# A block of two layers on one core: the second FFN's up-projection by Strassen's algorithm, in a written order

## The chip, the cores and the metric

The kernel runs on one core of a Trainium2 chip. The metric is the device time of one execution, in microseconds (us). The median of three runs before the change is 1634.23 us (1628.58 to 1636.04). The trace is that of one profiled execution, whose span from the first to the last instruction is 1633.7 us.

The engines are TensorE (PE in the profile; PEld is its weight load), VectorE (DVE), ScalarE (ACT), GpSimd (POOL), and SyncE (SP), whose queue issues the DMAs. Each engine works through its own list of instructions in order; semaphores tie the lists together.

## The reference

Two layers work on 512 tokens `x` and 256 context tokens `ctx`, 1024 features wide, in float32: a Fourier and Hyena mixer with an FFN, then latent attention with an FFN. The change touches the FFN of the second layer, and the norm ahead of it:

```python
D_MODEL, SEQ, D_FF = 1024, 512, 2816

def _conv_ffn(h, w_up, conv_w, conv_b, w_down):
    gate, val = jnp.split(h @ w_up, 2, axis=-1)
    return (jax.nn.silu(_dwconv3(gate, conv_w, conv_b)) * val) @ w_down
...
x = x + g1 * yx
x = x + g2 * _conv_ffn(_modulate(_rms_norm(x, norm2[i]), sh2, sc2), *ffn)
```

`_dwconv3` is a convolution of three taps over the tokens, feature by feature.

## The kernel before

Features lie on the 128 partitions, tokens on the free axis. `x`, `hh` and `hl` are lists of 8 tiles of 128 x 512. Precision is kept by splitting each operand of a matmul into a high part, rounded to the type fp32r by ScalarE (`hi`, line 131), and a low part, the difference, by VectorE (`lo`, line 137). `mm3` (lines 156 to 160) then runs three matmuls into one accumulator: high by high, weights' high by low, weights' low by high. Each has a weight tile of 128 x 128 of its own.

A weight tile comes by `wload`: a DMA of 128 x 1024 into `wr`, its high part into `wh`, its low part into `wl`. These three tags have three buffers each in the pool `W`, in turn; so a high part is made when TensorE is through with the tile that had the buffer. PSUM has three buffers of 1024 columns (`mm`) and two of 512 (`ms`).

The second FFN has 2816 = 22 x 128 hidden features. `up(f)` in `ffn` (line 1156) loads a gate tile and a value tile of weights, runs 8 x 2 `mm3` over the 8 tiles of `hh` and `hl` (48 matmuls of 512 columns), then the convolution on the gate straight from PSUM (lines 373 to 375, one ScalarE and two VectorE instructions), the Silu on ScalarE, the product with the value on VectorE, and the split into `ah` and `al`. For f = 0 the matmuls run in two halves of 256 tokens. The down-projection (`res_proj`, line 1102) comes in three groups of 8, 8 and 6 hidden tiles: for each of 8 output tiles a weight load, 24 or 18 matmuls of 512 columns, and one VectorE addition to `x` (line 1143). The first tile of the next group is computed ahead of each group.

Ahead of the FFN stands the attention's output projection, `res_proj` over two halves of 256 tokens, with weights loaded again for the second half where they were not kept. The norm of a half (`norm`, line 254) hangs on it by hooks: squares on ScalarE, their sum, `fold` (a matmul with ones), a reciprocal root on VectorE in twelve small steps, `spread` (a matmul that brings it to all partitions), and for each tile `scaled` (VectorE, then ScalarE with the bias, which writes `hh`) and `low` (VectorE, which writes `hl`).

In the mixer the order of the engines is written out by hand (`manual_schedule`); elsewhere, the second FFN among it, a scheduler sets the order on each engine by the order in the program and what is ready.

## Time and profile before

| | |
|---|---|
| median of three runs | 1634.23 us |
| the profiled execution's span | 1633.7 us |
| TensorE clock granted, mean | 0.989 |
| weights of the second FFN's up-projection | 44 loads of 512 KB |
| of its down-projection | 16 loads of 512 KB, 8 of 384 KB |
| landing of one such load after its issue | 3.0 to 3.3 us, median |

In a row of the timeline stand the start, the duration (both us), the engine, the line, the operation, the tile written and those read, the shape, and how many like it follow; in brackets, idle time of the engine before it and what ended that. TensorE's durations overlap, since matmuls are pipelined: its pace is the distance of two starts. The same holds for VectorE to a small degree. A group's row gives the count, then the busy time, the mean in ns, and idle time ahead. Times in the trace count from the span's start.

### The profile page before, as it was taken

To read this page: it belongs to the slowest core of one execution; us is meant where nothing else is said; L and a number is where in the kernel's file an instruction comes from. 1 tells how busy PE (TensorE), PEld (TensorE's weight loads), DVE (VectorE), ACT (ScalarE), POOL (GpSimd) and SP (SyncE) were. 2 spreads that over 40 slices of the span, in tenths; PEclk is the share of its full clock that TensorE was granted. 3 is DMA by queue.
4 is the path that set the end of the run, shared out by engine and by line. 5 is a ranking of instruction groups with operands and counts; after the bars stand their busy time and mean duration, and the time that the engine had idled before them with its cause. 6 is when DMAs were issued, how large, how long until landed. Compare 5 with 4: busy or idle time off the path is not lost.

```text
span 1633.7 us, 20802 instructions
## 1 busy us (share of the span) xinstructions
PE 1590.5 (97%) x8248; PEld 1300.4 (80%) x8248; DVE 1047.7 (64%) x1702; ACT 620.7 (38%) x883; POOL 109.5 (7%) x165
## 2 busy tenths in 40 slices
PE   7999998999999999999999989999999999999999
PEld 5787888888888888888888877666659888878887
...
PEclk9999998999999999999999998999999999999999
...
GB/s 361 109 105 231 156 29 78 192 118 112 159 155 117 77 129 145 164 104 77 113 160 86 83 70 1 13 11 14 0 99 147 78 103 92 90 104 90 90 91 90
DMA packets 54541, 173.35 MB, mean 106 GB/s; under 512 B 6187, under 2 KB 9453, under 8 KB 53421
## 3 DMA queue, kind: packets, MB, share of 16 engines
...
q8 instruction: 65, 1.06, 0.2%
...
## 4 chain that ended last, share of the span: by engine, by line
PE 81%; DVE 14%; issue 2%; ACT 1%; POOL 1%; DMA 1%; SPq 0%; POOLq 0%; DVEq 0%; ACTq 0%
PE mm L158 24%; PE mm L159 23%; PE mm L160 23%; PE pv L1611 2%; DVE wl L138 1%; DVE S L1587 1%; DVE junk L243 1%; PE s L1557 1%; DVE wr L1626 1%; PE k L158 1%; PE k L160 1%; PE k L159 1%; DVE hl L313 1%; PE mm L616 1%; DVE mx L1571 0%
## 5 line engine op out<-in xcount | busy, mean ns | idle before, releaser
L158 PE MATMUL mm<-hh,wh 128*128 128x512 f32 (+2 forms) x1360 | 481.7, 357 | 1.8 <-ACT wh L133 0.9
L159 PE MATMUL mm<-hl,wh 128*128 128x512 f32 (+2 forms) x1360 | 479.3, 353 | 2.3 <-DVE hl L313 2.3
L160 PE MATMUL mm<-hh,wl 128*128 128x512 f32 (+2 forms) x1360 | 478.7, 353 | 1.6 <-DVE wl L138 1.6
L133 ACT ACTIVATE wh<-wr 128x1024 fp32r<-128x1024 f32 (+1 forms) x192 | 197.8, 1033 | 571.1 <-PE mm L159 547.9
L138 DVE TENSOR_TENSOR wl<-wr,wh 128x1024 fp32r<-128x1024 f32 (+2 forms) x192 | 231.0, 1205 | 236.2 <-ACT wh L133 229.6
L158 PEld LDWEIGHTS mm<-hh,wh 128*128 128x128 f32 x1360 | 257.5, 190 | 48.7 <-issue 7.8
L159 PEld LDWEIGHTS mm<-hl,wh 128*128 128x128 f32 x1360 | 257.8, 190 | 39.0 <-DVE hl L313 3.5
L160 PEld LDWEIGHTS mm<-hh,wl 128*128 128x128 f32 x1360 | 257.6, 190 | 37.6 <-DVE wl L138 2.2
L243 DVE SCALAR_TENSOR_TENSOR junk<-wr,sb 128x1024 bf16<-128x1024 f32 x128 | 156.2, 1220 | 40.4 <-DMA wr<-wmodT 39.8
L158 PE MATMUL mm<-ah,wh 128*128 128x512 f32 (+1 forms) x480 | 172.4, 359 | 0.0
L160 PE MATMUL mm<-ah,wl 128*128 128x512 f32 (+1 forms) x480 | 172.2, 359 | 0.0
L159 PE MATMUL mm<-al,wh 128*128 128x512 f32 (+1 forms) x480 | 172.0, 359 | 0.0
L1143 DVE SCALAR_TENSOR_TENSOR xr<-mm,mod,xr 128x512 f32<-128x512 f32 (+1 forms) x100 | 61.7, 631 | 154.8 <-PE mm L160 153.1
L159 PEld LDWEIGHTS mm<-al,wh 128*128 128x128 f32 x480 | 90.5, 189 | 14.1 <-DVE al L138 0.2
L158 PEld LDWEIGHTS mm<-ah,wh 128*128 128x128 f32 x480 | 90.4, 188 | 14.2 <-issue 0.3
L160 PEld LDWEIGHTS mm<-ah,wl 128*128 128x128 f32 x480 | 90.4, 188 | 14.2
L1611 PE MATMUL pv<-S,V 128*128 128x512 f32 x192 | 93.9, 598 | 2.5 <-ACT S L1590 2.5
L1175 ACT ACTIVATE fg<-fg 128x772 f32<-128x772 f32 (+1 forms) x44 | 32.6, 741 | 97.7 <-DVE fg L375 90.9
L1565 ACT ACTIVATE S<-s,rks 128x512 f32<-128x512 f32 x96 | 62.6, 685 | 12.4 <-PE pv L1611 8.5
L1611 PEld LDWEIGHTS pv<-S,V 128*128 128x128 f32 x192 | 34.5, 190 | 34.7 <-issue 29.3
L1587 DVE TENSOR_TENSOR S<-S,mx 128x1536 f32<-128x1536 f32 x32 | 55.3, 1749 | 2.3 <-POOL mx L1583 2.3
L1583 POOL PARTITION_ALL_REDUCE mx<-mx x16 | 44.9, 2804 | 163.6 <-DVE mx L1580 163.6
...
## 6 DMA issues: line engine op xcount, KB each, us to landing
wr<-w_up SPq DMA_DIRECT2D x88, 512.0 KB, 3.2
wr<-wmodT SPq DMA_DIRECT2D x80, 512.0 KB, 3.2
wr<-w_dn SPq DMA_DIRECT2D x32, 512.0 KB, 3.3
...
wr<-w_in SPq DMA_DIRECT2D x16, 512.0 KB, 4.2
wr<-w_out SPq DMA_DIRECT2D x13, 512.0 KB, 3.3
...
wr<-w_o SPq DMA_DIRECT2D x11, 512.0 KB, 3.2
```

Of the source, the lines that this page charges most:

```text
L133: self.nc.scalar.activation(dst, src, AF.Copy)
L138: (eng or self.nc.vector).tensor_tensor(dst, src, hi.bitcast(F32), op=ALU.subtract)
L158: mmul(out, wh, xh, start=start, stop=False)
L159: mmul(out, wh, xl, start=False, stop=False)
L160: mmul(out, wl, xh, start=False, stop=stop)
L243: nc.vector.scalar_tensor_tensor(junk, raw, 1.0, self.sb[:, j, :], op0=ALU.mult, op1=ALU.mult, accum_out=acc)
L1143: nc.vector.scalar_tensor_tensor(x[m][:, a2:b2], ps[:, a2:b2], mod[:, 8 * sec + m, c : c + 1], x[m][:, a2:b2], op0=ALU.mult, op1=ALU.add)
L1175: nc.scalar.activation(g[:, :n], g[:, :n], AF.Silu)
L1565: nc.scalar.activation(c.S[a][j // 3][:, j % 3, :], c.ps[a, j], AF.Copy, scale=c.r[:, g : g + 1])
L1583: nc.gpsimd.partition_all_reduce(c.m[a][:, 1, :], c.m[a][:, 0, :], P, bass.bass_isa.ReduceOp.max)
L1587: v.tensor_tensor(c.S[a][h], c.S[a][h], mb.to_broadcast([P, 3, T]), op=ALU.subtract)
L1611: nc.tensor.matmul(c.P[a], V[:, j, o : o + 128], c.S[a][j // 3][:, j % 3, :], start=j == 0, stop=j == 5)
```

## The change

The first 2 of the 22 up tiles are computed as before. For the other 20, Strassen's algorithm takes the place of the 8 block products: the reduction is cut into two halves of 512 features (a), the tokens into two halves of 256 (b), and the outputs are gate (g) and value (v). Seven products `P1` to `P7` of 4 `mm3` each (12 matmuls of 256 columns) use sums of weight blocks and sums of blocks of the norm's result. The sums of weights (`S1` to `S4`, 512 columns each) are made by VectorE for each tile, then split (`Ha`, `La`, `Hb`, `Lb`). The sums of the norm's result (`T1` to `T4`, `Th`, `Tl`) are made once. For this `scaled` in `norm` writes the whole result, in float32, into "quarter" tiles first, by one more ScalarE instruction, and `hh` and `hl` from that. The products are added up by VectorE from PSUM (`C1` to `C4`, `Ua`, `Ub`, `Xv`, 256 columns each) with one copy by ScalarE (`K1`); gate and value then lie in SBUF.

All steps of this FFN stand in one written order, in which TensorE, VectorE, ScalarE and SP each take their steps as they come. A step's name ends in its up tile, or in its group and output tile. `R` is a DMA, `H` a high part, `L` a low part; `Ca`, `Cb`, `Cc` are the convolution, `Si` the Silu, `Ml` the product with the value, `Ah` and `Al` the split; `U1` is the second whole tile, `D` a down tile, `X` its addition to `x`. The down-projection is cut into five groups of 5, 5, 4, 4 and 4 hidden tiles, between the ups. The first two up weights are loaded in a hook of the output projection, ahead of the load for its last tile, m=4. The first whole tile U0 is run around the second half's norm, in the code ahead of the string.

On every engine the instructions up to the last loads of the output projection stand in the same order as before. TensorE has 720 matmuls more.

```diff
+UP_ORDER = """
+Rv2 Rg2 Rv3 Hv2 S1.2 T1 Hg2 U1 Ca0 Lv2 Th1 S2.2 Tl1 Ha2 T3 La2 Th3 T2 S3.2 Th2 Tl3 S4.2 Tl2 Hb2 Rg3 Cb0 Lb2 P1.2 Ca1 Cc0 P2.2 T4 K1.2 Si0 Lg2 P5.2 Th4
+C1.2 Rv4 Ml0 Hv3 P6.2 Tl4 Ah0 Lv3 P7.2 Ua2 S1.3 P1.3 Ub2 Xv2 C2.2 P4.2 K1.3 S2.3 S3.3 Ha3 P3.2 Cb1 Hg3 S4.3 La3 P2.3 Rg4 Hb3 Cc1 P5.3 Hv4 Lb3 Si1 P6.3
+C1.3 Lv4 P7.3 Ml1 Lg3 Ah1 P1.4 Ua3 Rv5 C3.2 Ub3 Xv3 P4.3 C2.3 S1.4 C4.2 P3.3 S2.4 Hg4 S3.4 K1.4 Ha4 Lg4 P2.4 S4.4 La4 Hb4 Rg5 Hv5 C1.4 P5.4 Lb4 Rv6 Lv5
+P6.4 Al0 P7.4 C3.3 Ca2 Ua4 S1.5 P1.5 Cb2 Ub4 Cc2 P4.4 Xv4 Si2 C2.4 S2.5 P3.4 Hg5 C4.3 Ml2 Ha5 P2.5 S3.5 K1.5 La5 Ah2 S4.5 P5.5 C1.5 Hb5 Rg6 Lg5 P6.5
+Al1 Hv6 Lb5 Rv7 Ca3 Lv6 P7.5 Ua5 Cb3 P1.6 Ub5 Cc3 P4.5 Xv5 Si3 C2.5 C3.4 S1.6 P3.5 Hg6 C4.4 S2.6 K1.6 P2.6 Ml3 Ha6 S3.6 Ah3 Lg6 La6 S4.6 P5.6 C1.6 Hb6
+Rg7 Al2 P6.6 C3.5 Hv7 Lb6 Rd0.0 Ca4 Lv7 P7.6 Ua6 Cb4 P1.7 Ub6 Cc4 P4.6 Xv6 Si4 C2.6 S1.7 P3.6 C4.5 Hg7 S2.7 K1.7 Ml4 Ha7 P2.7 S3.7 Ah4 Al3 La7 Ca5 S4.7
+P5.7 C1.7 Hb7 Rd0.1 Al4 P6.7 Lg7 Hd0.0 Lb7 Rd0.2 Hd0.1 Ld0.0 P7.7 Ua7 Rv8 Cb5 D0.0 Xv7 Cc5 Ub7 Si5 C4.6 C2.7 Ca6 Ld0.1 C3.6 Rg8 P4.7 Ml5 X0.0 Ah5 Cb6
+P3.7 C4.7 Cc6 Hg8 D0.1 S1.8 Si6 S3.8 Hd0.2 S2.8 Hv8 Ld0.2 Lv8 Rd0.3 D0.2 S4.8 Ha8 X0.1 Rd0.4 La8 Lg8 C3.7 Rv9 P1.8 Ml6 Hb8 X0.2 Ah6 P2.8 Al5 K1.8 Lb8
+Ca7 P5.8 Hd0.3 C1.8 Cb7 Ld0.3 P6.8 Cc7 Rg9 Al6 P7.8 Si7 Ua8 Hd0.4 Ml7 D0.3 Xv8 Ah7 Ub8 Ld0.4 C2.8 Rd0.5 S1.9 S3.9 S2.9 P4.8 Al7 S4.9 P3.8 X0.3 Hg9 C4.8
+Lg9 Ca8 D0.4 C3.8 Hv9 Cb8 Ha9 Cc8 Lv9 Si8 La9 Rd0.6 P1.9 Hb9 Rd0.7 X0.4 P2.9 Lb9 K1.9 Ml8 P5.9 Hd0.5 C1.9 Ah8 Ld0.5 P6.9 Al8 Rv10 P7.9 Hd0.6 Ua9 Xv9
+Ld0.6 D0.5 Ub9 Rg10 C2.9 S1.10 P4.9 X0.5 S2.10 P3.9 S3.10 Hg10 C4.9 S4.10 Ca9 D0.6 Lg10 Hd0.7 C3.9 Hv10 Ld0.7 Cb9 Rv11 Lv10 D0.7 Ha10 X0.6 Rg11 Cc9
+La10 Si9 Rv12 Ml9 S1.11 P1.10 Ah9 X0.7 Hb10 S2.11 P2.10 K1.10 Lb10 P5.10 Al9 Hv11 C1.10 S3.11 P6.10 Lv11 P7.10 S4.11 Ha11 Ua10 Rg12 Xv10 P1.11 La11
+Ub10 P4.10 K1.11 C2.10 S1.12 P3.10 S2.12 Hg11 C4.10 Lg11 Ca10 P2.11 C3.10 Hb11 Rd1.0 Cb10 P5.11 Cc10 Hv12 Lb11 Si10 P6.11 C1.11 Lv12 P7.11 Ha12 Ua11
+S3.12 P1.12 Xv11 Ub11 La12 P4.11 K1.12 C2.11 S4.12 P3.11 Ml10 Hg12 Rd1.1 C4.11 Ah10 Lg12 P2.12 Ca11 C3.11 Rd1.2 Hb12 Cb11 Al10 P5.12 Hd1.0 Lb12 P6.12
+C1.12 Ld1.0 P7.12 Cc11 Rd1.3 Hd1.1 Ua12 Si11 Ld1.1 D1.0 Ub12 Rv13 Xv12 C2.12 Ml11 Ah11 Al11 P4.12 X1.0 P3.12 C4.12 Ca12 D1.1 Cb12 Hd1.2 C3.12 Hd1.3
...
+Al21 D3.7 Hd4.1 X3.6 Ld4.1 Rd4.4 D4.0 Hd4.2 X3.7 Ld4.2 Rd4.5 D4.1 Hd4.3 X4.0 Ld4.3 Rd4.6 D4.2 Hd4.4 X4.1 Ld4.4 Rd4.7 D4.3 Hd4.5 X4.2 Ld4.5 D4.4 Hd4.6
+X4.3 Ld4.6 D4.5 Hd4.7 X4.4 Ld4.7 D4.6 X4.5 D4.7 X4.6 X4.7
+"""
+UP_GROUPS = ((0, 5), (5, 10), (10, 14), (14, 18), (18, 22))
+UP_WHOLE = 2
...
         def scaled(d):
             A, B = self.A[i][k][:, j, :], self.mod[i][:, 24 * k : 24 * k + 8, j]
+            if whole is not None:
+                u = box[d] = whole(d)
+                nc.vector.scalar_tensor_tensor(u, x[d][:, c0 : c0 + n], A[:, d : d + 1], box["R"][:, :n], op0=ALU.mult, op1=ALU.mult)
+                nc.scalar.activation(u, u, AF.Identity, bias=B[:, d : d + 1])
+                return nc.scalar.activation(hh[d][:, c0 : c0 + n], u, AF.Copy)
...
+        def whook(stage, j, m):
+            hook(stage, j, m)
+            if stage and j == 6:
+                first.extend(self.wload(I["w_up"][1, 0, q]) for q in range(2))
...
-        self.ffn(1, x, hh, hl, T, [(0, T)], half, None)
+        self.ffn_blocks(x, hh, hl, quarter, first, rest.steps)
...
+        def S1(f):
+            s, g = self.t(bl, [P, 1024], F32, "sum"), k_["rg", f]
+            k_["sa", f] = s
+            v.tensor_tensor(s[:, 512:1024], g[:, 0:512], g[:, 512:1024], op=ALU.add)
...
+        def prod(ps, w, o, mov):
+            for q in range(4):
+                s = slice(o + 128 * q, o + 128 * q + 128)
+                self.mm3(ps, w[0][:, s], w[1][:, s], *mov(q), q == 0, q == 3)
...
+        def P1(f):
+            m = k_["m", f] = self.mm()
+            prod(m[:, 0:256], k_["wv", f], 0, part(0, 0))
+        def P2(f):
+            prod(k_["m", f][:, 512:768], k_["wv", f], 512, part(1, 0))
+        def P5(f):
+            b = k_["b", f] = self.ms()
+            prod(b[:, 0:256], k_["wa", f], 512, tf(1))
+        def P6(f):
+            prod(k_["m", f][:, 0:256], k_["wa", f], 0, tf(2))
+        def P7(f):
+            prod(k_["m", f][:, 512:768], k_["wb", f], 512, tf(3))
+        def P4(f):
+            prod(k_["m", f][:, 0:256], k_["wg", f], 0, tf(4))
+        def P3(f):
+            prod(k_["b", f][:, 0:256], k_["wb", f], 0, part(1, 1))
+        def K1(f):
+            k_["t", f] = self.t(bl, [P, 3, 256], F32, "t")
+            nc.scalar.copy(k_["t", f][:, 0, :], k_["m", f][:, 0:256])
...
+        def C1(f):
+            k_["v", f] = self.t(tm, [P, T], F32, "fv", 3)
+            plus(k_["v", f][:, 0:256], k_["t", f][:, 0, :], k_["m", f][:, 512:768])
+        def Ua(f):
+            plus(k_["t", f][:, 1, :], k_["t", f][:, 0, :], k_["m", f][:, 0:256])
+        def Ub(f):
+            plus(k_["t", f][:, 2, :], k_["t", f][:, 1, :], k_["m", f][:, 512:768])
+        def Xv(f):
+            plus(k_["v", f][:, 256:512], k_["t", f][:, 1, :], k_["b", f][:, 0:256])
+        def C2(f):
+            k_["g", f] = self.t(tm, [P, T], F32, "fg")
+            minus(k_["g", f][:, 256:512], k_["t", f][:, 2, :], k_["b", f][:, 0:256])
...
+        with self.tc.manual_schedule(engines={ENG.PE, ENG.DVE, ENG.Activation, ENG.SP}):
+            k_["wg", 0], k_["wv", 0] = first
+            take(KD)
+            Rv(1)
+            Rg(1)
+            Hv(1)
+            Hg(1)
+            U_(0, [(0, 256)], (0, 1))
+            f2(False, 0)
+            U_(0, [(0, 256)], (2, 3, 4, 5))
+            Lv(1)
+            Lg(1)
+            f2(False, 1)
+            U_(0, [(0, 256)], (6, 7))
+            for d in range(KD + 1):
+                if d < KD:
+                    a2(d, 0)
+                if d:
+                    a2(d - 1, 1)
+            U_(0, [(256, 256)], range(KD))
+            for s in UP_ORDER.split():
+                step(s)
```

More of the change, by code (lines that the diff above doesn't have):

```diff
@@ L251, in make_A, with norm @@
             self.nc.vector.scalar_tensor_tensor(self.A[i][k][:, j, a:b], sc, 1.0, self.pcol[:, o + a : o + b], op0=ALU.add, op1=ALU.mult)
-    def norm(self, i, k, x, hh, hl, c0, n, tp):
+    def norm(self, i, k, x, hh, hl, c0, n, tp, whole=None):
         nc = self.nc
@@ L311, in low @@
         def low(d):
+            if whole is not None:
+                return nc.vector.tensor_tensor(hl[d][:, c0 : c0 + n], box.pop(d), hh[d][:, c0 : c0 + n].bitcast(F32), op=ALU.subtract)
             B = self.mod[i][:, 24 * k : 24 * k + 8, j]
@@ L1717, in layer1 @@
         self.xp = self.pool("xres")
[L1718 removed]
+        tp = lambda: self.t(nt, [P, 256], F32, "nt")
         x = [self.t(self.xp, [P, T], F32, f"xr{d}") for d in range(KD)]
@@ L1728, in layer1 @@
         hl = [self.t(hp, [P, T], F32R, f"hl{d}") for d in range(KD)]
-        hook, rest = self.norm_hook(*[self.norm(1, 1, x, hh, hl, c, 256, tp) for c in (0, 256)])
-        self.res_proj(1, 2, oh, ol, KD, lambda m: I["w_o"][m], x, half, hook, ready=2)
-        rest()
+        quarter = [[None] * 2 for _ in range(2)]
+        for a, b in ((0, 0), (0, 1), (1, 1), (1, 0)):
+            quarter[a][b] = self.t(self.xp, [P, 4, 256], F32, "quarter", 5)
+        whole = lambda b: lambda d: quarter[d // 4][b][:, d % 4, :]
+        hook, rest = self.norm_hook(*[self.norm(1, 1, x, hh, hl, 256 * b, 256, tp, whole(b)) for b in range(2)])
+        first = []
+        def whook(stage, j, m):
+            hook(stage, j, m)
+            if stage and j == 6:
+                first.extend(self.wload(I["w_up"][1, 0, q]) for q in range(2))
+        self.res_proj(1, 2, oh, ol, KD, lambda m: I["w_o"][m], x, half, whook, ready=2)
         self.close("pO")
```

177 lines of the change are left out of this document (176 added, 1 removed).

## The prediction

> **What bounds the kernel now.** I read the page first, then the stretches of the second FFN, then single rows of TensorE and VectorE there.
>
> ```profile
> span 1633.7 us, 20802 instructions
> ...
> PE 1590.5 (97%) x8248; PEld 1300.4 (80%) x8248; DVE 1047.7 (64%) x1702; ACT 620.7 (38%) x883; POOL 109.5 (7%) x165
> ...
> PE   7999998999999999999999989999999999999999
> ...
> PEclk9999998999999999999999998999999999999999
> ...
> PE 81%; DVE 14%; issue 2%; ACT 1%; POOL 1%; DMA 1%; SPq 0%; POOLq 0%; DVEq 0%; ACTq 0%
> ```
>
> TensorE is busy 97% of the span and holds 81% of the chain that ended last. In the second FFN it is the bound outright; in the table of stretches (span, then TensorE, weight loads, VectorE, ScalarE, GpSimd busy, clock, DMA share, GB/s) the first row is the stretch after the first up tile, the next two are one up tile each:
>
> ```profile
> 1276.00:1630.30 354.30, 353.83 (x1526) 285.43 (x1524) 151.20 (x177) 106.48 (x130) 0.00 (x0) 1.00 0.28 95
> ...
> 1311.15:1322.31 11.16, 11.16 (x50) 8.95 (x49) 5.06 (x6) 3.94 (x6) 0.00 (x0) 1.00 0.27 94
> 1322.31:1333.47 11.16, 11.16 (x50) 8.95 (x49) 5.06 (x6) 3.94 (x6) 0.00 (x0) 1.00 0.27 96
> ```
>
> TensorE has no gap in 354 us, while VectorE works 151 us and ScalarE 106. An up tile is 48 matmuls of 512 columns and takes 11.16 us, VectorE 5.06 us of it. So less TensorE work shortens this stage one for one, until VectorE is asked for more than TensorE takes.
>
> **The change, part by part. Matmuls.** Twenty up tiles go from 48 matmuls of 512 columns to 7 products of 12 matmuls of 256. Such matmuls run already in the attention output projection; these are the first and the last of 97 rows in a row:
>
> ```profile
> 1229.01 0.28 PE L158 MATMUL mm<-Oh,wh 128*128 128x256 f32 x1
> ...
> 1240.41 0.28 PE L158 MATMUL mm<-Oh,wh 128*128 128x256 f32 x1
> ```
>
> 11.40 us over 96 steps is 0.1187 us each, with the borders between weight tiles in it. 84 of them are 9.97 us (one product 1.425), so a tile saves 1.19 and twenty save **23.8 us**. The down-projection keeps its 528 matmuls of 512 columns; eight tiles per group become eight tiles in each of five shorter groups. Its pace, by the starts of the additions that end two neighbouring tiles of 24 matmuls in the first and in the second group:
>
> ```profile
> 1374.27 0.75 DVE L1143 SCALAR_TENSOR_TENSOR xr<-mm,mod,xr 128x512 f32<-128x512 f32 x1 [2.92 <-PE mm L160]
> ...
> 1379.87 0.75 DVE L1143 SCALAR_TENSOR_TENSOR xr<-mm,mod,xr 128x512 f32<-128x512 f32 x1 [3.52 <-PE mm L160]
> ...
> 1502.63 0.75 DVE L1143 SCALAR_TENSOR_TENSOR xr<-mm,mod,xr 128x512 f32<-128x512 f32 x1 [0.19 <-PE mm L160]
> ...
> 1508.12 0.75 DVE L1143 SCALAR_TENSOR_TENSOR xr<-mm,mod,xr 128x512 f32<-128x512 f32 x1 [2.80 <-PE mm L160]
> ```
>
> 5.60 and 5.49 us, a mean of 0.231 us a matmul; the sum is 122 us before and after, and costs nothing new.
>
> **VectorE.** A Strassen tile adds four weight sums, three 1024-wide low parts instead of two (and one of 512), and seven additions of 256 columns out of PSUM. What counts is the step from one instruction to the next when VectorE has a queue:
>
> ```profile
> 1256.13 0.48 DVE L1143 SCALAR_TENSOR_TENSOR xr<-mm,mod,xr 128x256 f32<-128x256 f32 x1
> 1256.53 0.47 DVE L308 SCALAR_TENSOR_TENSOR nt<-xr,A,ms 128x256 f32<-128x256 f32 x1
> ...
> 1258.51 0.42 DVE L274 TENSOR_TENSOR nt<-nt,nt 128x256 f32<-128x256 f32 x1
> 1258.85 1.22 DVE L138 TENSOR_TENSOR wl<-wr,wh 128x1024 fp32r<-128x1024 f32 x1
> ...
> 1260.06 1.22 DVE L138 TENSOR_TENSOR wl<-wr,wh 128x1024 fp32r<-128x1024 f32 x1
> 1261.19 0.15 DVE L283 SCALAR_TENSOR_TENSOR nrm_s<-ms,nrm_s 128x2 f32<-128x2 f32 x1
> ...
> 1281.94 0.69 DVE L1177 TENSOR_TENSOR fg<-fg,mm 128x512 f32<-128x512 f32 x1 [0.72 <-ACT fg L1175]
> 1282.61 0.75 DVE L374 SCALAR_TENSOR_TENSOR fg<-mm,pcol,fg 128x511 f32<-128x511 f32 x1
> 1283.39 0.69 DVE L138 TENSOR_TENSOR al<-fg,ah 128x512 fp32r<-128x512 f32 x1
> 1284.00 0.74 DVE L375 SCALAR_TENSOR_TENSOR fg<-mm,pcol,fg 128x511 f32<-128x511 f32 x1
> ```
>
> So 256 columns step 0.40 from PSUM and 0.34 from SBUF, 1024 from SBUF 1.135, 512 from PSUM 0.665, 512 from SBUF 0.605 (640 columns, in between, 0.74). A tile is 3 x 1.135 + 9 x 0.605 (four sums, one low part, two convolution taps, the product, its low part) + 7 x 0.40 = **11.65 us on VectorE against 9.97 on TensorE**. A down tile is the reverse: 1.3 to 1.4 us on VectorE, 12 or 15 matmuls, 2.8 or 3.5 us, on TensorE. Hence, where ups follow each other without downs, VectorE sets the pace. I sum both engines along the written order. Ahead of the product P7.7 (tile 7, the last before the first down tile) TensorE has U1 and 39 products: 11.16 + 39 x 1.425 = 66.7 us. It needs Lb7, and VectorE has up to there 26 x 1.135 + 44 x 0.605 + 6 x 0.665 + 34 x 0.40 = 73.7 us. TensorE must have waited 7.0 us by then. The same sum gives 3.1 at P7.5, 4.9 at P5.6, 6.8 at P1.9, and only 2.7 at P7.12 (147.0 against 144.3); it turns negative from the second group of downs (D1.1) on: there TensorE is the bound again. VectorE's whole list is 300 us against TensorE's 333. VectorE starts its list about 0.7 us ahead (six 256-wide matmuls of U0 follow its last norm step), so this term is 7.0 - 0.7, and the wake-up brings it to **+7**. With 256 columns at 0.34 it would be 5 - 0.7; the other end is under the rivals.
>
> **The start.** The norm writes its result first as a whole (quarter tiles) and needs one more ScalarE step per tile, and the first up weights are fetched ahead of the last output-projection tile, m=4.
>
> ```profile
> 1256.01 1.06 ACT L133 ACTIVATE wh<-wr 128x1024 fp32r<-128x1024 f32 x1 [0.38 <-PE mm L159]
> ...
> 1256.28 0.28 PE L159 MATMUL mm<-hl,wh 128*128 128x256 f32 x1
> 1258.19 0.38 PE L160 MATMUL mm<-hh,wl 128*128 128x256 f32 x1 [1.63 <-DVE wl L138]
> ...
> 1266.87 1.31 ACT L309 ACTIVATE hh<-nt,mod 128x256 fp32r<-128x256 f32 x3 [8.79 <-DVE nt L308]
> ...
> 1267.42 0.74 PE L158 MATMUL mm<-hh,wh 128*128 128x256 f32 x3 [0.88 <-ACT hh L309]
> ```
>
> A high part waits for its buffer, which TensorE frees (first row). In the new order it is m=4 whose buffer comes free only when TensorE is through with m=3, so the wait of 1.63 us moves ahead of m=4 and becomes about 2.3 (1.06 for the high part, 1.135 for the low one, 0.1 to start); after it U0 finds its weights ready, which puts U0 0.4 us later. ScalarE's steps of 256 columns come 0.4 us apart (1.31 for three); two per tile are 0.8 to 0.9 against the 0.71 that six matmuls take, eight times, less the 1.4 us of matmuls that now cover the 0.88 us wait: +0.6. Sum **+1**; bounds 0 and 4 (every extra ScalarE step of 0.5 us uncovered).
>
> **Hand-offs.** P6, P7, P4 and P3 overwrite PSUM that ScalarE or VectorE must have read; each of the 140 products may find its release just in time. What that costs, beside the usual 0.23:
>
> ```profile
> 1310.84 0.40 PE L160 MATMUL mm<-hh,wl 128*128 128x512 f32 x1
> ...
> 1311.15 0.47 PE L158 MATMUL mm<-hh,wh 128*128 128x512 f32 x1
> ```
>
> 0.31 instead of 0.23, so 0.08; 140 x 0.08 = 11 above, 0 below (the 97 rows cross four borders at no cost). While VectorE paces, it is inside that term; afterwards VectorE is ahead. I take a quarter, **+3**. Queued behind a waiting C1, Ua or C2 on VectorE are the next low parts, and behind those TensorE: this is what the 3 pays for.
>
> **No cost:** ScalarE (per tile three steps of 1.06 and five shorter ones, under 8.5 us of 9.97). SP issues 32 DMAs more (16 more down tiles, 16 cut in two) for the same bytes, at a DMA share of 0.27; a load lands in 3.2 us:
>
> ```profile
> wr<-w_up SPq DMA_DIRECT2D x88, 512.0 KB, 3.2
> ```
>
> Between the issue Rg6 and its reader S1.6 VectorE has eleven steps, 6.7 us. Should a wr buffer come free that late, all loads behind it in SP's queue wait too, and each costs up to its 3.2 us.
>
> Sum: 1633.7 - 23.8 + 7 + 1 + 3 = 1620.9 for the profiled execution, which lies 0.5 under the median of 1634.2: **1621 us**. Its own range: products 1% quicker (-2), VectorE 4.3, the rest 0: 1612; VectorE 10, hand-offs 6, start 2: 1628.
>
> **Rivals. 1: VectorE takes the durations, not the steps (slower).** Steps count if instructions overlap; where one needs the last one's result or another engine's, its whole duration counts.
>
> ```profile
> L138 DVE TENSOR_TENSOR wl<-wr,wh 128x1024 fp32r<-128x1024 f32 x71 | 87.6, 1234 | 110.7 <-ACT wh L133 109.1
> ...
> L374 DVE SCALAR_TENSOR_TENSOR fg<-mm,pcol,fg 128x511 f32<-128x511 f32 x22 | 16.4, 744 | 0.0
> L138 DVE TENSOR_TENSOR al<-fg,ah 128x512 fp32r<-128x512 f32 x22 | 15.2, 692 | 13.3 <-ACT ah L133 13.3
> ...
> L1143 DVE SCALAR_TENSOR_TENSOR xr<-mm,mod,xr 128x256 f32<-128x256 f32 x12 | 5.8, 482 | 4.3 <-PE mm L160 4.2
> ```
>
> Up to C1.12 VectorE has 41, 94, 14 and 71 instructions of the four kinds and 8 of 640 columns: 41 x 1.234 + 94 x 0.692 + 14 x 0.744 + 71 x 0.482 + 8 x 0.82 = 167 against 144 on TensorE, a wait of 23 instead of 7: 1637; with 0.03 us between dependent ones (228 x 0.03 = 7) 1644. It decides from 0.077 us more on each of the 228 on. For it: chains S1-S2, Ua-Ub and Cb-Cc depend. Against: the order puts other work between them, and the rows above overlap by 0.09. The Trainium skill (VectorE: DVE Perf Modes, Terms) says that the pipe is drained after every operation and the next can't issue until it is empty; by that rule this rival would be the forecast. The trace does not agree: the 1.22 us row at 1260.06 ends at 1261.28, and the next starts at 1261.19.
>
> **2: Hand-offs at their full price**, 11 instead of 3: 1629. Against: VectorE leads by 14 us at D3.0.
>
> **3: The clock.** After short waits it has halved:
>
> ```profile
> 1260.00:1264.00 4.00, 4.00 (x22) 4.00 (x23) 3.13 (x15) 0.00 (x0) 0.00 (x0) 0.57 0.77 266
> ...
> 970.00:983.00 13.00, 9.56 (x65) 7.67 (x65) 9.65 (x23) 5.99 (x10) 2.83 (x6) 1.00 0.18 61
> 983.00:994.00 11.00, 11.00 (x41) 8.70 (x40) 3.52 (x8) 3.02 (x6) 0.82 (x1) 0.53 0.01 1
> ```
>
> A stretch of half clock costs 4.0 x 0.43 = 1.7 us, the long one 5.2. The waits of the new order reach 1.8 us at a time (P7.5 to P5.6). Three such stretches of 1.7: 1626; one long one beside them: 1631. Against: most of it falls where VectorE paces. The Trainium skill (TensorE: Matmul & The Clock Gate, "HAM oscillation") has the clock halve only after idle gaps over some 3.4 us, which would rule this out; the trace shows it after a gap of 1.63.
>
> **4: 256 columns are bound by the weight loads**, so that the change doesn't save what it says: at 0.19 us a load a tile is 84 x 0.19 = 16 us, 20 x 4.8 = 96 us slower. The 97 rows at 0.1187 rule it out for this form.
>
> **Numbers.** This kernel's measurement can tell about 0.5%, 8.2 us: 1626.0 and 1642.4. Forecast (1612 to 1628) 0.67; hand-offs 0.08; clock 0.07; VectorE's durations 0.17; the rest 0.01. Faster: the forecast but for 0.02, and half of the clock, 0.69; same: that 0.02, the hand-offs, the other half of the clock and half of rival 1, 0.21; slower: the other half of rival 1 and the rest, 0.10. The range reaches from 1612 to 1634, over rivals 2 and 3; rival 1 and the rest, 0.18, are left out.
>
> **What would show it.** Right: P products at 0.117 to 0.120 a matmul; TensorE's waits on VectorE (La, Lb, Lv) of some 7 us between U1 and D0.4, few after D1.1; clock 1.00 but for one short stretch near 1260; VectorE steps as above. Wrong: waits on VectorE in the third to fifth group, VectorE's 256-column additions over 0.47 a step, or a product pitch over 0.125.

## The result and the profile after

The changed kernel takes 1639.26 us (median of 7 runs, 1637.11 to 1642.77), the kernel before 1634.15 beside it: a ratio of 1.0039 with a 95% interval of 1.0023 to 1.0054. It is slower by 0.4%, where the prediction said 1621. The page of the changed kernel, in the lines that answer to those of before (busy time by engine, the clock in slices, the chain that ended last):

```profile
span 1639.6 us, 22741 instructions
...
PE 1573.3 (96%) x8968; PEld 1317.5 (80%) x8968; DVE 1197.0 (73%) x2003; ACT 672.2 (41%) x980; POOL 109.0 (7%) x165
...
PEclk9999998999999999999999999999999999999999
...
PE 67%; DVE 22%; DMA 4%; issue 3%; ACT 3%; POOL 1%; SPq 0%; POOLq 0%; DVEq 0%; ACTq 0%
```

TensorE is busy 17.2 us less than before, and yet the span is 5.9 us longer. Its share of the chain that ended last has fallen from 81% to 67%, VectorE's has risen from 14% to 22%. The time was saved and given back as waits. Three rows of the timeline cut the changed kernel into pieces: the high part of the output projection's tile m=2 (the last place up to which nothing differs), the first matmul of U1, and the last matmul.

```profile
1243.23 1.06 ACT L172 ACTIVATE wh<-wr 128x1024 fp32r<-128x1024 f32 x1 [1.74 <-PE mm L198]
...
1281.84 0.40 PE L197 MATMUL mm<-hh,ah 128*128 128x512 f32 x1
...
1635.16 0.40 PE L199 MATMUL mm<-ah,wl 128*128 128x512 f32 x1
```

The same places in the kernel before (U1's first matmul has no record; its second is the middle row, so U1 began near 1274.1):

```profile
1240.84 1.06 ACT L133 ACTIVATE wh<-wr 128x1024 fp32r<-128x1024 f32 x1 [1.74 <-PE mm L159]
...
1274.30 0.40 PE L159 MATMUL mm<-hl,wh 128*128 128x512 f32 x1
...
1629.44 0.39 PE L160 MATMUL mm<-ah,wl 128*128 128x512 f32 x1
```

| piece | before | after | difference | predicted |
|---|---|---|---|---|
| up to the mark (no edit there) | 1240.8 | 1243.2 | +2.4 | 0 |
| **start**: mark to U1 | 33.3 | 38.6 | +5.3 | +1 |
| **FFN**: U1 to the last matmul | 355.3 | 353.3 | -2.0 | -13.8 |
| behind it | 4.3 | 4.4 | +0.2 | 0 |

The first row differs from run to run: in the kernels below, which have the same code up to there, the mark lies between 1239.0 and 1244.1.

In the FFN the products themselves are quicker than predicted. One that nothing holds up takes 1.36 or 1.41 us from its start to the next one's, on average 1.38. U1 (11.0) and 528 matmuls of the down tiles (121.1), at the pace of before of 0.2293, and 140 products (193.2) make 325.3 us. The stage took 353.3: **28.0 us are waits**. I call this the excess; for one step it is the distance to the next step's start beyond 1.38. Ahead of product 6 it sums to 11.3 us, ahead of product 4 to 5.8, ahead of product 7 to 5.8. The 11.3 hold 3.2 us in which product 5, once started, waited for its own low part (the row with `ms` below). Here is what TensorE waited for from U1 on (engine, tile and line, releaser: us in total, times, longest):

```profile
PE mm L197 <- DVE fv L1931: 8.3, 12, 1.4
PE ms L199 <- DVE wl L177: 3.2, 4, 1.2
PE mm L197 <- DVE t L1931: 2.9, 5, 1.0
PE mm L199 <- DVE wl L177: 1.3, 4, 0.5
PE mm L197 <- ACT wh L172: 0.6, 1, 0.6
```

The prediction expected the rows with `wl`, the low parts. The largest row is another: `fv` at line 1931 is C1, the sum of products 1 and 2. No product reads it. Five of the 12 waits, 3.0 us, are product 7's, which overwrites product 2 and so must wait until C1 has read that. The other seven, 5.3 us, are product 6's. The timeline of tile 10 shows one of these:

```profile
1413.36 0.68 DVE L1874 TENSOR_TENSOR sum<-sum,wr 128x512 f32<-128x512 f32 x1
1413.70 0.35 ACT L1928 COPY t<-mm 128x256 f32<-128x256 f32 x1
1413.95 1.22 DVE L177 TENSOR_TENSOR wl<-sum,wh 128x1024 fp32r<-128x1024 f32 x1
1414.44 0.28 PE L199 MATMUL ms<-th,wl 128*128 128x256 f32 x1
1415.09 0.69 DVE L177 TENSOR_TENSOR al<-fq,ah 128x512 fp32r<-128x512 f32 x1
1415.69 0.42 DVE L1931 TENSOR_TENSOR fv<-t,mm 128x256 f32<-128x256 f32 x1
1416.02 0.69 DVE L1878 TENSOR_TENSOR sum<-wr,wr 128x512 f32<-128x512 f32 x1
1416.16 0.38 PE L197 MATMUL mm<-th,wh 128*128 128x256 f32 x1 [1.44 <-DVE fv L1931]
```

Product 5 ends with the matmul at 1414.44. Product 6 overwrites product 1's columns, which K1 had copied at 1413.70 already. But it starts only when C1 has run, and C1 reads product 2 from the other half of the same PSUM tile `mm`. C1 itself could have run at 1414.1, with K1 done; it stood behind S2, Lb and Al in VectorE's written order. Product 4 and Ub are the same case: Ub reads product 7's half, product 4 writes the other (the row `t`, 2.9 us, each time released by Ub).

### The profile page after: what moved, and what is told of

It is laid out like the page before. It is cut to its first block, busy times and chain, and to the rows that moved or that the text cites. A ratio compares the mean times of both kernels' runs of the same rounds, so it can differ in the third digit from the quotient of the medians.

```text
span 1639.6 us, 22741 instructions
## 1 busy us (share of the span) xinstructions
PE 1573.3 (96%) x8968; PEld 1317.5 (80%) x8968; DVE 1197.0 (73%) x2003; ACT 672.2 (41%) x980; POOL 109.0 (7%) x165
## 4 chain that ended last, share of the span: by engine, by line
PE 67%; DVE 22%; DMA 4%; issue 3%; ACT 3%; POOL 1%; SPq 0%; POOLq 0%; DVEq 0%; ACTq 0%
PE mm L197 19%; PE mm L198 18%; PE mm L199 18%; DVE wl L177 4%; DMA wr<-w_up 2%; PE pv L1657 2%; DVE junk L282 2%; DVE S L1633 2%; PE s L1603 1%; DVE wr L1672 1%; DMA wr<-wmodT 1%; ACT wh L172 1%; DVE fv L1931 1%; PE ms L199 1%; PE ms L197 1%
## 5 line engine op out<-in xcount | busy, mean ns | idle before, releaser
L197 PE MATMUL mm<-hh,wh 128*128 128x512 f32 (+2 forms) x1192 | 395.8, 334 | 2.9 <-ACT hh L350 1.4
L198 PE MATMUL mm<-hl,wh 128*128 128x512 f32 (+2 forms) x1192 | 394.6, 332 | 2.5 <-DVE hl L359 2.3
L199 PE MATMUL mm<-hh,wl 128*128 128x512 f32 (+2 forms) x1192 | 393.9, 331 | 1.0 <-DVE wl L177 1.0
L172 ACT ACTIVATE wh<-wr 128x1024 fp32r<-128x1024 f32 (+3 forms) x187 | 177.7, 957 | 422.0 <-PE mm L198 383.1
L177 DVE TENSOR_TENSOR wl<-wr,wh 128x1024 fp32r<-128x1024 f32 (+3 forms) x187 | 207.3, 1114 | 120.6 <-ACT wh L172 120.0
L197 PEld LDWEIGHTS mm<-hh,wh 128*128 128x128 f32 x1192 | 225.2, 189 | 32.4 <-issue 3.1
L198 PEld LDWEIGHTS mm<-hl,wh 128*128 128x128 f32 x1192 | 225.0, 189 | 27.6 <-DVE hl L359 3.3
L199 PEld LDWEIGHTS mm<-hh,wl 128*128 128x128 f32 x1192 | 224.8, 189 | 23.3 <-DVE wl L177 1.8
L1189 DVE SCALAR_TENSOR_TENSOR xr<-mm,mod,xr 128x512 f32<-128x512 f32 (+1 forms) x76 | 43.7, 594 | 90.6 <-PE mm L199 89.0
L197 PEld LDWEIGHTS mm<-ah,wh 128*128 128x128 f32 x480 | 90.2, 188 | 13.3
L172 ACT ACTIVATE wh<-sum 128x1024 fp32r<-128x1024 f32 x40 | 42.3, 1058 | 33.6 <-PE mm L198 15.3
```

Source lines behind the costliest of these rows:

```text
L172: self.nc.scalar.activation(dst, src, AF.Copy)
L177: (eng or self.nc.vector).tensor_tensor(dst, src, hi.bitcast(F32), op=ALU.subtract)
L197: mmul(out, wh, xh, start=start, stop=False)
L198: mmul(out, wh, xl, start=False, stop=False)
L199: mmul(out, wl, xh, start=False, stop=stop)
L1189: nc.vector.scalar_tensor_tensor(x[m][:, a2:b2], ps[:, a2:b2], mod[:, 8 * sec + m, c : c + 1], x[m][:, a2:b2], op0=ALU.mult, op1=ALU.add)
```

## The experiments

**Theory A**: the semaphores go by whole PSUM tiles, so that products 6 and 4 wait for readers of the other half. **Rival B**: VectorE has simply too much to do, and whatever releases TensorE comes late. **Rival C**: every hand-off costs a wake-up. For the start: the early weights, or the norm's second ScalarE step.

All times are medians; ratio and 95% interval are against the kernel before on the same chip, the excess is that of the profiled execution. In five of these the granted clock halved within the FFN, for 3.4 us each time: twice in e3 and e7, once in e6, e9 and e11. By an estimate (half of 3.4) each costs 1.7 us, which is in the excess.

| run | us | ratio | interval | excess, us |
|---|---|---|---|---|
| changed kernel | 1639.26 | 1.0039 | 1.0023 to 1.0054 | 28.0 |
| e1_split | 1620.18 | 0.9908 | 0.9889 to 0.9926 | 10.3 |
| e2_late | 1635.15 | 0.9998 | 0.9988 to 1.0009 | 26.9 |
| e3_al_twice | 1652.18 | 1.0099 | 1.0084 to 1.0114 | 40.6 |
| e4_pool34 | 1644.28 | 1.0044 | 1.0029 to 1.0059 | 30.6 |
| e5_split_late | 1616.15 | 0.9894 | 0.9877 to 0.9910 | 9.4 |
| e6_split_al_twice | 1632.82 | 0.9983 | 0.9970 to 0.9996 | 22.3 |
| e7_c1_after_p6 | 1647.28 | 1.0073 | 1.0048 to 1.0098 | 35.5 |
| e8_best_lows | 1619.79 | 0.9905 | 0.9889 to 0.9922 | 9.9 |
| e9_split_p2 | 1628.28 | 0.9966 | 0.9954 to 0.9979 | 19.3 |
| e10_nobias | 1615.25 | 0.9891 | 0.9871 to 0.9911 | 9.8 |
| e11_whole3 | 1617.11 | 0.9900 | 0.9884 to 0.9916 | 11.3 |
| e12_whole3_order | 1618.33 | 0.9892 | 0.9872 to 0.9911 | 10.9 |
| e13_whole3_wg2 | 1616.79 | 0.9887 | 0.9868 to 0.9906 | 9.1 |
| e14_split_late_wg2 | 1616.91 | 0.9888 | 0.9869 to 0.9908 | 9.6 |

### e1: two PSUM tiles where there was one

```diff
+        self.mm = lambda: self.t(self.ps, [P, 512], F32, "mm", 3)
+        self.mv = lambda: self.t(self.ps, [P, 512], F32, "mv", 3)
...
         def P2(f):
-            prod(k_["m", f][:, 512:768], k_["wv", f], 512, part(1, 0))
+            k_["n", f] = self.mv()
+            prod(k_["n", f][:, 0:256], k_["wv", f], 512, part(1, 0))
...
-            prod(k_["m", f][:, 512:768], k_["wb", f], 512, tf(3))
+            prod(k_["n", f][:, 0:256], k_["wb", f], 512, tf(3))
```

The PSUM space is the same; C1, Ub, the whole tiles' value and its readers follow.

> Only the PSUM tiles change: products 1, 6 and 4 (and the gate, the down tiles, the output projection) take tiles of 512 columns, products 2 and 7 (and the value) tiles of their own. Theory A (whole-tile waits: product 6 waits for C1, which reads only product 2's half of the tile, and product 4 for Ub, which reads only product 7's): TensorE's excess ahead of products 6 and 4, 17 us in the changed kernel, falls below 9, and the time falls by 5 to 12 us, to 1627 to 1634. Rival B (VectorE's load alone sets the excess): the low parts are just as late, the excess moves to other products, and the time stays within 2 us of 1639. Rival C (the price is the wake-up of each hand-off): as B, since the hand-offs remain.

The time fell by 19 us, more than Theory A's own figure. The waits of the split kernel from U1 on:

```profile
PE ms L199 <- DVE wl L177: 3.0, 3, 1.3
PE mv L197 <- DVE fv L1934: 1.5, 3, 0.8
PE mm L199 <- DVE wl L177: 0.9, 1, 0.9
PE mv L199 <- DVE wl L177: 0.4, 2, 0.2
```

The wait for C1 is left only where it is real (product 7 into `mv`), and the wait for `t` is gone; the low parts' rows are nearly what they were. Product 6 of tile 10 now starts while C1 still runs, 0.11 us behind the last matmul of product 5:

```profile
1406.36 0.28 PE L199 MATMUL ms<-th,wl 128*128 128x256 f32 x1
1406.42 0.42 DVE L1934 TENSOR_TENSOR fv<-t,mv 128x256 f32<-128x256 f32 x1
1406.47 0.28 PE L197 MATMUL mm<-th,wh 128*128 128x256 f32 x1
```

The excess ahead of products 6 and 4 fell from 17.1 to 5.9 us. A rival would be that the split only gives more buffers. It would show ahead of products 1 and 2, which take new ones, and there the excess fell by 1.3 us only (2.4 to 1.1). The waits that the shared tile makes without need (5.3 us of product 6 for C1, 2.9 of product 4 for Ub) don't hold the whole gain of 17.7. For the rest I have an argument and no measurement: a product that starts late also delays what VectorE takes from it, and VectorE in its fixed order then delays the next low part. The table of stretches shows where it went (from U1 to D0.0, from there to D1.0, from there to the end; columns as in the prediction), first the changed kernel:

```profile
1281.84:1358.56 76.72, 70.81 (x531) 65.95 (x529) 72.17 (x110) 40.52 (x53) 0.00 (x0) 1.00 0.23 75
1358.56:1442.29 83.73, 78.58 (x542) 71.71 (x541) 74.14 (x119) 37.01 (x53) 0.00 (x0) 1.00 0.30 95
1442.29:1635.40 193.11, 187.45 (x1190) 167.92 (x1188) 152.37 (x245) 75.19 (x107) 0.00 (x0) 1.00 0.32 100
```

and the split one:

```profile
1278.94:1352.29 73.35, 69.07 (x530) 65.30 (x529) 72.42 (x112) 40.08 (x53) 0.00 (x0) 1.00 0.24 78
1352.29:1429.41 77.12, 76.69 (x542) 71.45 (x541) 73.00 (x120) 37.65 (x53) 0.00 (x0) 1.00 0.32 103
1429.41:1614.72 185.31, 184.12 (x1190) 166.57 (x1188) 151.31 (x245) 75.45 (x107) 0.00 (x0) 1.00 0.33 105
```

The gains are 3.4, 6.6 and 7.8 us: most lies where VectorE is not the bound. In the first stretch VectorE (the third of the busy times) now works 72.4 of 73.4 us. That is its pace, and 7.1 of the 10.3 us of excess that are left stand there.

### e9 and e7: which half, and whether an order would do

In e9 product 2 has its own tile and product 7 shares one with products 1, 6 and 4 (Ub follows). In e7 the tiles are those of the changed kernel, and C1 is written behind product 6.

```diff
 # e9, against e1
-            prod(k_["n", f][:, 0:256], k_["wb", f], 512, tf(3))
+            prod(k_["m", f][:, 256:512], k_["wb", f], 512, tf(3))
...
 # e7, against the changed kernel (tile 10 as an example)
-P5.10 Al9 Hv11 C1.10 S3.11 P6.10 Lv11 P7.10
+P5.10 Al9 Hv11 S3.11 P6.10 C1.10 Lv11 P7.10
```

> Half of the split: product 2 has a tile of its own, product 7 shares one with products 1, 6 and 4. So products 6 and 7 no longer wait for C1, while product 4 still waits for Ub, which reads product 7, and Ua still waits for product 7. If both shared halves matter by the excess measured ahead of their products in the changed kernel (11 us ahead of product 6, 6 ahead of product 4): 1625 to 1631, with the excess ahead of product 4 still 4 to 6 us. If only C1 and product 6 matter: 1619 to 1622. If only Ub and product 4: 1634 or more.

> Shared PSUM tiles as in the changed kernel; in the written order C1 is moved behind product 6 in the 14 tiles where it stood ahead of it. Theory A: product 6 no longer waits for C1, but C1 now waits for product 6, which writes the tile that it reads, and product 7 waits for C1: the excess of 11 us ahead of product 6 moves ahead of product 7, and the time stays within 4 us of 1639. Rival (only the place of C1 in VectorE's order was wrong): 6 to 10 us less, 1629 to 1633.

e9 came in between, as Theory A has it: 1628, with the excess ahead of product 6 down to 4.6 us, and that ahead of product 4 still there (8.5, where 4 to 6 was expected), released by `t`:

```profile
PE mm L197 <- DVE t L1934: 3.7, 6, 1.4
```

So both halves count, 9 to 10 us for product 2's and 7 to 9 for product 7's (an excess of 28.0, 19.3 and 10.3; the lower or higher figure depends on whether the 1.7 us of halved clock in e9 are taken off). In e7 the excess did move, from ahead of product 6 (11.3 to 2.8) to ahead of product 7 (5.8 to 15.1). C1 is still the largest releaser (first row), and it itself now waits for TensorE (second row; 5.1 us in 6 waits in the changed kernel):

```profile
PE mm L195 <- DVE fv L1929: 10.1, 17, 0.7
DVE fv L1929 <- PE mm L197: 13.9, 15, 1.7
```

It cost 8 us, where I had expected at most 4. By the same rule C1, now written behind product 6, has to wait for a product whose result it doesn't need, and VectorE's next steps with it. A part of the 8 us is the clock: from U1 to D0.0 it was 0.96 in the profiled execution, and the one execution of e7 with 0.993 over the whole took 1641.4 us. With a shared tile neither place for C1 gained anything.

### e3 and e6: what VectorE's work costs

In both, each up tile's low part of the activations is computed twice; the result is the same.

```diff
         def Al(f):
-            self.lo(acts[f][1], k_["q", f], acts[f][0])
+            for _ in range(2):
+                self.lo(acts[f][1], k_["q", f], acts[f][0])
```

> Each up tile's low part of the activations is computed twice by VectorE (22 x 0.605 = 13.3 us more VectorE work, the result unchanged): VectorE's price in this stage. Theory A (VectorE paces only up to the end of the first group of tiles, and after that TensorE waits for single results): the time rises by 3 to 6 us, to 1642 to 1645. Rival B (VectorE's load sets the excess throughout): it rises by 10 to 13, to 1649 to 1653. If nothing waits for VectorE: 0.

> The doubled low part of the activations (13.3 us more VectorE work) on the kernel with split PSUM tiles. On the shared tiles it cost its whole price, 12.9 us. Theory D (the shared tile closed a loop: TensorE waits for VectorE's next steps, VectorE in its written order waits for TensorE's next product, so all VectorE work stands on the path; the split opens the loop and VectorE paces only up to the first down tile, ahead of which stand five of the 22 repeats): the time rises by 3 to 6 us, to 1623 to 1626. Rival B (VectorE's load is on the path in any case, the split only saved wake-ups): by 10 to 13, to 1630 to 1633.

12.9 us on the shared tiles and 12.6 on the split ones, for 13.3 us of work: **this is rival B's number, and theory D fell.** A part is the clock again. The executions of e6 with a mean clock of 0.992 or 0.993 took 1627.8 to 1628.9 us, those with 0.985 took 1634.2 to 1636.3. At a like clock (0.989) e6 took 1631.2 and e1 1619.8. That is still far above theory D's 3 to 6. The split takes waits away, but doesn't make TensorE less sensitive to VectorE's work. The stretches of e6 show why in part:

```profile
1281.97:1358.77 76.80, 69.10 (x530) 65.35 (x529) 75.69 (x117) 40.49 (x53) 0.00 (x0) 1.00 0.23 75
1358.77:1441.18 82.41, 79.34 (x542) 73.19 (x541) 77.29 (x125) 37.14 (x52) 0.00 (x0) 0.98 0.31 97
```

The first stretch grew by 3.5 us and the second by 5.3. If with the added work VectorE sets the pace up to D1.0, not only up to D0.0, eleven repeats, 6.7 us, count there; a clock of 0.98 in the second row is another 1.6 us; the two stretches grew by 8.7. That adding work may also move the point up to which it counts is what I had overlooked. No run tests it, and VectorE still idles for 5 us in the second row. The 3.3 us by which the third stretch grew aren't explained by this: VectorE has 30 us to spare there.

### e2, e5, e10, e8: the start

e2 fetches the first up weights after the last output-projection tile. e5 does so in the split kernel. e10 adds to e5 that the norm's second ScalarE step, and so the shift of the normalised activations, is left out. e8 adds to e5 that two low parts, which stood ahead of the norm's scalings, come between them.

```diff
 # e2, e5
-            if stage and j == 6:
+            if stage and j == 7:
                 first.extend(self.wload(I["w_up"][1, 0, q]) for q in range(2))
...
 # e10, against e5
-                nc.scalar.activation(u, u, AF.Identity, bias=B[:, d : d + 1])
...
 # e8, against e5
-            Lv(1)
-            Lg(1)
             f2(False, 1)
...
                     a2(d - 1, 1)
+                {3: Lv, 6: Lg}.get(d, len)((1, [])[d not in (3, 6)])
```

> The first up weights are fetched after the last output-projection tile again, as before the change; nothing else. Theory A (the start costs 6 us, most of it since the two loads, high and low parts of 1024 columns stand ahead of tile m=4's in the queues of ScalarE and VectorE): the wait of 5 us ahead of m=4 shrinks to 2 or 3, and the time falls by 3 to 4 us, to 1635 to 1636. Rival (the start is late because of the norm's second ScalarE step): the time stays within 1 us of 1639.

> Both edits together: own PSUM tiles for products 2 and 7, and the first up weights fetched after the last output-projection tile. If the two terms are separate (the start ends before the up tiles begin): 19 and 4 us below the changed kernel, 1614 to 1617. Rival (what the start gives back is lost in the first group, where VectorE still paces): 1618 to 1621.

> The kernel with split tiles and late weights, and the norm's second ScalarE step left out (the shift isn't added to the normalised activations: another result). It prices that step alone. Theory (of the 6 us that the start lost, 3 to 4 were the early weights, the rest is the step: the scaled tiles came 0.92 us apart where six matmuls take 0.71): 1.5 to 2.5 us less than the kernel with the two edits. Rival (the chain is set by VectorE's two steps a tile): within 0.7 us of it.

> As the kernel with split tiles and the late weights, and the two low parts of tile 1's weights, which stood on VectorE between the norm's square root and its first scaling, moved behind the scalings of tiles 2 and 5. If they hold up the norm's chain (in the changed kernel the first scaling came 1.9 us after the row that spreads the root): 1 to 2 us less than with the two edits alone. Rival (the next tile's low parts are only shifted, and U1 or the other scalings wait for them): the same or up to 2 us more.

In the changed kernel, ahead of m=4, these rows explain the wait (the first two are ScalarE's high parts of the second up weight and of m=4):

```profile
1256.14 1.04 ACT L172 ACTIVATE wh<-wr 128x1024 fp32r<-128x1024 f32 x1
1257.39 1.04 ACT L172 ACTIVATE wh<-wr 128x1024 fp32r<-128x1024 f32 x1
1258.49 0.39 PE L197 MATMUL mm<-Oh,wh 128*128 128x256 f32 x1 [2.81 <-ACT wh L172]
1260.51 0.58 PE L199 MATMUL mm<-Oh,wl 128*128 128x256 f32 x1 [1.52 <-DVE wl L177]
```

TensorE waits 2.81 us for m=4's high part, which stands behind the up weights' on ScalarE, and soon 1.52 for its low part, which stands behind theirs on VectorE. In e2 one wait is left:

```profile
1254.25 0.38 PE L199 MATMUL mm<-Oh,wl 128*128 128x256 f32 x1 [2.00 <-DVE wl L177]
```

From the mark to U1 it is 35.2 us in e2, after 38.6: 3.4 less. But this distance also depends on how long the clock is halved there, which differs between kernels with the same code up to U1. The rows below go from the mark to U1 (first the span, third from the end the clock). They are the changed kernel, e1 with the same code; then e5, e14 with the same code; then e10:

```profile
1243.23:1281.84 38.61, 32.77 (x238) 30.88 (x237) 30.02 (x79) 22.75 (x49) 0.00 (x0) 0.91 0.30 96
1241.36:1278.94 37.58, 31.67 (x238) 29.88 (x236) 29.91 (x79) 22.73 (x49) 0.00 (x0) 0.95 0.32 99
...
1244.14:1279.10 34.96, 31.42 (x238) 29.79 (x236) 29.82 (x79) 22.66 (x49) 0.00 (x0) 0.95 0.34 106
1240.41:1273.88 33.47, 29.93 (x237) 28.33 (x236) 29.71 (x79) 22.73 (x49) 0.00 (x0) 1.00 0.34 111
...
1243.78:1276.98 33.20, 30.23 (x238) 29.57 (x236) 29.36 (x79) 16.14 (x33) 0.00 (x0) 0.95 0.35 112
```

At the same clock of 0.95 the early weights cost 2.6 us (37.6 in e1, 35.0 in e5) and the norm's step 1.8 (33.2 in e10). The kernel before, also at 0.95, has 33.3. The changed kernel's profiled execution had its clock halved for longer than e1's, and lies 1.0 above it. Together that is 5.4 us, for the 5.3 of the start. The step shows behind the halved clock too: from the beginning of the wait for the first scaled tile to U1 it is 8.9 us in e5 and in e14, and 7.0 in e10.

In the medians e2 gave 4 us. e5's median lies 4 us under that of the split alone, but their intervals overlap; e10's 0.9 is within the scatter, and for this step only the trace speaks. e8 did not gain the 1 to 2 us: it takes 36.1 from the mark to U1 at the same clock as e5's 35.0, with two new waits for `hl`, 0.88 and 0.96, as its rival had it; its median is 3.6 us higher, within the intervals.

### e4: two of the four sums on GpSimd

```diff
-            v.tensor_tensor(s[:, 512:1024], k_["rg", f][:, 0:512], k_["rv", f][:, 0:512], op=ALU.add)
+            nc.gpsimd.tensor_tensor(s[:, 512:1024], k_["rg", f][:, 0:512], k_["rv", f][:, 0:512], op=ALU.add)
```

S4 likewise; GpSimd's steps join the written order.

> The third and fourth weight sums of every tile (40 of 80) run on GpSimd, which is idle in this stage; 24 us less VectorE work, 8 us of it in the first group. Theory A: VectorE's pace in the first group is relieved (its excess is 10.5 us), the waits through the shared PSUM tile stay: -4 to -8, to 1631 to 1635. Rival B: -12 to -20, to 1619 to 1627. Against both: a GpSimd sum of 512 columns takes 1.45 us (row of the page) instead of 0.69, two in a row 2.9, and product 7 may wait for it: then 0 or slower.

It got 5 us slower, as the last sentence allowed, but the rows show a further reason. The groups of e4 (busy us, mean ns, idle ahead):

```profile
L1878 POOL TENSOR_TENSOR sum<-wr,wr 128x512 f32<-128x512 f32 x19 | 32.2, 1697 | 208.1 <-DMA wr<-w_up 136.2 <-DVE wl L177 59.3 <-DVE fq L1972 12.7
L177 DVE TENSOR_TENSOR wl<-wr,wh 128x1024 fp32r<-128x1024 f32 x19 | 31.3, 1647 | 0.1
L1931 DVE TENSOR_TENSOR t<-t,mm 128x256 f32<-128x256 f32 x40 | 16.6, 415 | 14.8 <-PE mm L199 14.6
```

and of the changed kernel:

```profile
L177 DVE TENSOR_TENSOR wl<-wr,wh 128x1024 fp32r<-128x1024 f32 x19 | 23.2, 1221 | 0.2
L1931 DVE TENSOR_TENSOR t<-t,mm 128x256 f32<-128x256 f32 x40 | 16.7, 418 | 15.6 <-PE mm L199 15.5
```

VectorE's low parts of the value's weights became a third longer in the mean, 1221 to 1647 ns, and its additions out of PSUM not at all. It depends on whether a GpSimd sum runs at the same time. Of 20 such low parts 14 ran beside one and lasted 1801 ns, the other six 1218. Of the 40 low parts of sums only six did, and their mean rose little (1222 to 1246). So the relief was paid back on VectorE itself: from U1 to the end it is busy for 298.6 us, after 298.7, though 40 sums have left it. The Trainium skill (SBUF — State Buffer, "SBUF: two separate sides") says that a VectorE operation with two inputs in SBUF and a GpSimd operation that reads SBUF exclude each other for a whole instruction. The two rows agree with it, the one with two inputs in SBUF (1221 to 1647 ns) and the one with an input in PSUM (418 and 415).

### e11 to e14: can VectorE's pace in the first stretch be bought off

e11 makes tile 2 whole (no sums and no products). e12 writes the steps around it in another order. e13 adds a second buffer for the gate's split weights, and e14 that buffer to e5 alone.

```diff
 # e11, against e5; the steps of tile 2 in the string follow
-UP_WHOLE = 2
+UP_WHOLE = 3
...
 # e12, against e11: the region behind U2
-S1.3 P1.3 K1.3 S2.3 S3.3 Ca2 Ha3 Cb1 Hg3 S4.3 Cb2 La3 Cc2 P2.3 Rg4 Hb3
+S1.3 S2.3 Ha3 P1.3 Cb1 S3.3 La3 Hg3 S4.3 Cc1 Rg4 P2.3 K1.3 Hb3
...
 # e13 and e14
-H("wg", f, k_["rg", f][:, 512:1024], [self.t(bl, [P, 512], F32R, f"wg{q}", 1) for q in "hl"])
+H("wg", f, k_["rg", f][:, 512:1024], [self.t(bl, [P, 512], F32R, f"wg{q}", 2) for q in "hl"])
```

> The kernel with split tiles and late weights, and tile 2 whole too (48 matmuls of 512 columns, as tiles 0 and 1): TensorE 1.4 us more (11.0 against 7 x 1.38), VectorE 6 us less ahead of the first down tile. Theory (VectorE paces the first group; its excess there is 7.0 us): the excess of that group falls to 1 to 2.5 us and the time by 3 to 4.5, to 1612 to 1613.5. Rival (the waits of the first group are single late results, not VectorE's sum): 1 to 2 us slower than with tile 2 by products, 1617 to 1618.

> Tile 2 whole as in the run before it, with the steps of tiles 1 to 3 around it written in another order: there Ca2, which has to wait for the end of U2, stood ahead of Ha3 on ScalarE and Cb2 ahead of La3 on VectorE, and VectorE lost 3.2 us to it; now Ha3, La3, Hb3 and Lb3 stand ahead of them. Theory (VectorE's sum paces the first group, and its lead of some 5 us after U2 can be kept): the excess before the first down tile falls from 7.0 us to 1 to 3, the time to 1611.5 to 1614. Rival (the lead can't be kept, since a high part waits for one of three weight buffers, which TensorE frees, and the low part for the high part): the excess of products 5.6, 5.7 and 7.7 stays at 3 to 4 us, the time at 1615 to 1617.

> The kernel with tile 2 whole and the other written order, with two buffers instead of one for the high and low parts of the gate's weights of a product tile. Theory (ScalarE's queue stood at the single buffer, 6.17 us once, and VectorE's lead was lost behind it; with it gone VectorE's sum decides): the excess before the first down tile falls from 7.4 us to 2 to 4, the time to 1612 to 1615. Rival (other late steps take its place): 7 us, 1616 to 1618.

> The kernel with split tiles and late weights, with the same two buffers. Theory (there VectorE is busy 72.5 of the 73.3 us of the first group, so its sum is the bound and the buffer costs nothing): within 1 us of 1616. Rival (the buffer's wait is on the path there too): 2 to 4 us less.

None differs from e5 by more than its interval. In e11 to e13 the expected 3 us did not come; e14 stayed within 1 us, as its theory had it. The excess ahead of the first down tile stayed at 9.5 us (1.7 of it halved clock), 7.4 and 6.7 in e11 to e13, against 7.0 in e5. In e12 the gate's high part held ScalarE, and VectorE behind it:

```profile
1320.96 0.63 ACT L169 ACTIVATE wgh<-wr 128x512 fp32r<-128x512 f32 x1 [6.17 <-PE mm L195]
...
1322.58 1.22 DVE L174 TENSOR_TENSOR wl<-sum,wh 128x1024 fp32r<-128x1024 f32 x1 [1.77 <-ACT wh L169]
```

With two buffers (e13) this wait of VectorE is 0.27 us, and the time still the same. What the trace of e13 shows is that VectorE doesn't get ahead: from the start of U1 into tile 3's products it stands idle for 0.72, 1.57, 0.90, 0.26 and 1.65 us, each time for ScalarE, and from there on it loses 1.6 us a tile again (11.3 us of steps against 7 x 1.38). A written order that would keep its lead was not found.

## Why the prediction was wrong, by its own steps

**Matmuls, -23.8: right, and too small.** Products take 1.36 or 1.41 us instead of 1.425, which makes -30. A rival is settled with it: the loads of the weights don't bound 256 columns.

**VectorE, +7: right.** The split kernel shows 7.1 us ahead of the first down tile. It was hidden beneath another term. That it came out so exactly is partly luck. With the measured steps (in the rows of tile 10: 1.14 from 1413.95, 0.60 from 1415.09, and for 256 columns 0.33 from 1415.69, where 0.40 was taken; the taps 0.66 where 0.605 was) VectorE has 71.6 us ahead of P7.7 instead of 73.7, and with the quicker products TensorE 64.8 instead of 66.7: both sums were some 2 us too high, and their difference stayed. **Rival 1** (durations count) falls with these rows. The rule of the Trainium skill that was weighed there (VectorE: DVE Perf Modes, Terms) isn't borne out: the low part at 1413.95 lasts 1.22 us, and the next operation starts after 1.14.

**Hand-offs, +3: the step that failed.** It said that products 6, 7, 4 and 3 "overwrite PSUM that ScalarE or VectorE must have read", and priced the wake-up at 0.08 us each. It did not ask *which* instruction releases each product. By the columns, product 6 needs K1 alone, and product 4 Ua. In fact product 6 waits for C1, and product 4 for Ub. Those stand behind low parts and sums in VectorE's order, and only one product covers them instead of two. This is 17.7 us of excess (e1), with a good part from each half (e9). Without it the sum comes near: in the split kernel all stretches but the first have 3.2 us of excess. But the one wait that shows there, 1.5 us, is product 7's for C1 in VectorE's queue, so no run confirms the price of a wake-up. Its last sentence named what queues "behind a waiting C1"; it missed what C1 itself stands behind.

**The start, +1: mis-sized, 5.3.** The prediction let only the wait for the buffer move ahead of m=4 (2.3 us). It left out the two high parts and two low parts that the early loads put ahead of m=4's on ScalarE and VectorE: 2.6 us at the same clock (e1 and e5). The norm's extra step, taken at 0.6, is 1.8 (e10). The other 1.0 goes with the longer halved clock of that execution (0.91 against 0.95).

**Sum.** The profiled execution lies 18.7 us above the predicted one: 17.7 for the shared tile, 4.3 for the start, 2.4 ahead of the mark and 0.5 for small differences, less 6.2 for the quicker products. With the shared tile mended (e1), the kernel takes 1620 us. That this is so near the forecast of 1621 is luck: the start's 4.3 us and the products' 6.2 nearly cancel.

**Rival 2** (wake-ups at full price, 1629) names the right place, but the mechanism is not the wake-up: e1 has the same hand-offs and, behind the first stretch, 3.2 us. **Rival 3** (the clock) did not occur in the changed kernel's FFN, whose stretches have 1.00; in e3, e6, e7, e9 and e11 it did. At the start there is one stretch, longer than foreseen:

```profile
1260.00:1267.00 7.00, 6.49 (x33) 6.49 (x34) 2.26 (x6) 1.79 (x4) 0.00 (x0) 0.55 0.55 191
```

Of the signs named in advance, the waits on VectorE in the third to fifth group (behind D1.0 the changed kernel has 9.6 us of excess) told against the forecast at once.
